# Holding back weight conversions and delaying squares in a seven-product feed-forward stage

## The chip, the cores and the metric

The kernel runs on 1 core of one Trainium2 chip. The metric is the device time of one execution in microseconds (us); the time of the kernel before is the median of three runs.

## The reference

Two groups of tokens (128 prompt tokens and 512 latent tokens, 640 in all, model width 1024) pass through two layers that share their weights:

```python
mod = silu(cond) @ w_ada + b_ada                  # shift, scale, gate for mixer and FFN
h = rmsnorm(x, g_pre_mix) * (1 + sc1) + sh1
z = h @ w_in                                      # all mixers' inputs and four branch gates
merged = sum(sigmoid(g[b]) * branch[b] for b in "ABCD")   # conv, pooling, short conv, attention
x = x + gt1 * rmsnorm(merged @ w_o, g_post_mix)
h = rmsnorm(x, g_pre_ffn) * (1 + sc2) + sh2
f = square(relu(h @ w_ff1)) @ w_ff2               # w_ff1 is 1024 x 4096
x = x + gt2 * rmsnorm(f, g_post_ffn)
```

All inputs are float32.

## The kernel before

**Precision by splitting.** Each float32 operand is held as a high part (a cast to the matmul type) and a low part (the rest), and each product is three matmuls: high x high, high x low, low x high (`mm3`, L247 to L256). For a weight, the high part `wh` is a ScalarE cast of the raw tile `wr` (L188) and the low part `wl` is a VectorE subtraction (L197). PE takes these two in that order: its first two matmuls of a block need `wh` alone, the third needs `wl`; where the weights are the moving operand (QKV and the `nat` products, L250 to L252) the second needs `wl`.

**Weight supply.** Weights come in units of 128x1024 through three raw buffers (`N_RAW`) and are converted into four sets of `wh` and `wl` (`N_SETS`). `w_pump` casts sets up to three ahead of the one in use (`SPLIT_AHEAD`) as far as sets are free, and notes each cast in the list `w_late`; `w_low` takes from that list and emits the low part and whatever follows from it. `w_pump` is called where a set is taken (`w_next`) and where one is given back (`w_done`). `w_low(1)` is called at the end of every `tick`, which also hands VectorE and ScalarE work of the side generators (convolution, attention, modulation) between PE's products. In `w_pump` a raw tile whose own or whose predecessor's low part is still in `w_late` first has that low part emitted, at once:

```python
while any(x[1] in (u, u - 1) for x in self.w_late):
    self.w_low(1)
```

The order of emission is the order on each engine; the queues are in order.

**Stages of a layer.** QKV blocks (two units each, three blocks); twelve *sections* (`section`, L1022: one unit, two halves of 24 matmuls of 320 columns each, and an evacuation after each half); the gate and branch products of four branches (`gp`, `bp`); `merged @ w_o` (`nat`); and the feed-forward in four quarters. A section is

```python
u, st = self.w_next()
for h in range(2):
    ps = self.mmps("sec")
    self.ws_half(ps, st, h, hi, lo)
    fn(h, slice(h * HALF, h * HALF + HALF), ps[:, :HALF])
    self.tick(1.76, KN['sec'])
self.w_done(u)
```

**The seven products.** The first quarter of the FFN is multiplied plainly. The other three (`ffn_pairs`, L1185; six calls in the program) form two 128-column blocks of w_ff1 for both token halves with seven products in place of eight, four such pairs per call. A pair takes four sets, here A to D: A serves products 1 and 2, B products 7 and 3, C (two halves, C1 and C2) products 5 and 6, D product 4. The sets C and D hold sums of weight blocks: two sums follow A's low part (L202, L203), one follows C1's (L205), one C2's (L208), and a set whose raw tile is such a sum can only be cast after it. After product 6 VectorE combines results in five operations (L1219 to L1223) into `U`; after product 4 one more finishes `R` (L1226). `square` is three ScalarE operations on 128x640 (Relu, Square, cast to `ghi`; L1195 to L1197), `low` a VectorE one (`glo`, L1202).

Of the kernel before, what the change touches and what calls it, by code (L numbers as in the profile page):

```python
# [24 lines left out]
SPLIT_AHEAD = 3  # L25
# [39 lines left out]
def r32(ap):  # L65
    return ap.bitcast(F32)
# [9 lines left out]
class Kernel:  # L76
# [95 lines left out]
    def w_pump(self, upto):  # L172
        nc = self.nc
        while self.w_split < len(self.parts) and self.parts[self.w_split][0] <= upto:
            i, c, u, rc, then = self.parts[self.w_split]
            if i not in self.w_set:
                if self.w_live >= N_SETS:
                    break
                self.w_set[i] = [self.wp.tile([128, 1024], F32R, tag=n, name=self.nm(n), bufs=N_SETS) for n in ("wh", "wl")]
                self.w_live += 1  # L180
            if u not in self.w_raw:
                self.w_low()
            while any(x[1] in (u, u - 1) for x in self.w_late):
                self.w_low(1)
            self.w_fetch(u)
            raw = self.w_raw[u][:, rc]
            hi, lo = [w[:, c] for w in self.w_set[i]]
            nc.scalar.copy(hi, raw)  # L188
            self.w_late.append((self.w_split, u, raw, hi, lo, then))
            self.w_split += 1  # L190
# [994 lines left out]
    def ffn_pairs(self, hi, lo, S, ghi, glo):  # L1185

        nc = self.nc
        v = nc.vector.tensor_tensor
        p, q = slice(0, HALF), slice(HALF, NTOK)
        acts = {1: [(hi[k][:, p], lo[k][:, p]) for k in range(4)], 2: [(hi[k][:, p], lo[k][:, p]) for k in range(4, 8)],  # L1190
                4: [(hi[k][:, q], lo[k][:, q]) for k in range(4, 8)], 3: S[4], 5: S[1], 6: S[2], 7: S[3]}
        late = []

        def square(j, x):
            nc.scalar.activation(x, x, AF.Relu)  # L1195
            nc.scalar.activation(x, x, AF.Square)
            nc.scalar.copy(ghi[j], x)  # L1197
            late.append((j, x))

        def low():  # L1200
            j, x = late.pop(0)
            v(glo[j], x, r32(ghi[j]), ALU.subtract)  # L1202

        for pr in range(4):
            U, R = self.T("u"), self.T("r")
            ps = {}
            for ns in ((1, 2), (7, 3), (5, 6), (4,)):
                u, st = self.w_next()
                for i, n in enumerate(ns):
                    w = ps[n] = (self.sdps if n in (7, 3, 5) else self.mmps)("ffp")[:, :HALF]  # L1210
                    for k in range(4):
                        c = slice(i * 512 + k * 128, i * 512 + k * 128 + 128)
                        self.mm3(w, st[0][:, c], st[1][:, c], *acts[n][k], k == 0, k == 3)
                    if n == 1:
                        nc.scalar.copy(U[:, p], w)
                    elif n == 2:
                        v(R[:, p], w, U[:, p], ALU.add)
                    elif n == 6:
                        v(U[:, p], w, U[:, p], ALU.add)  # L1219
                        v(R[:, q], ps[7], U[:, p], ALU.add)  # L1220
                        v(U[:, q], ps[5], R[:, q], ALU.subtract)
                        v(U[:, p], ps[5], U[:, p], ALU.subtract)
                        v(U[:, p], ps[3], U[:, p], ALU.add)  # L1223
                        square(2 * pr + 1, U)
                    elif n == 4:
                        v(R[:, q], w, R[:, q], ALU.add)  # L1226
                        square(2 * pr, R)
                    if late and n in (2, 3):
                        low()
                    self.credit = -1.0  # L1230
                    self.tick(0, 0)
                self.w_done(u)
        while late:
            low()
        self.credit = 0.0
# [287 lines left out]
```

## Time and profile before

| | before |
|---|---|
| median of 3 runs | 2097.64 us (2095.79 to 2099.55) |
| the profiled execution | 2097.92 us |
| its span, first to last instruction | 2096.2 us |
| PE busy | 2013.9 us (96%) |
| VectorE (DVE) busy | 1487.6 us (71%) |
| ScalarE (ACT) busy | 867.7 us (41%) |
| granted TensorE clock, mean | 0.988 |

The profile gives, for each engine, busy time and what it waited for. A matmul's duration overlaps with its successor's, so a gap in PE's work is read from the waits and the starts, and a stage's cost from the stretch between its first matmul and the first of the next stage.

### The profile page before, as it was taken

How to read it: one execution, taken by the hardware profiler on the slowest of the kernel's cores; microseconds unless marked ns; L12 is line 12 of the kernel's file. 1: busy time of each engine (PE TensorE's matmuls, PEld its weight loads, DVE VectorE, ACT ScalarE, POOL GpSimd, SP SyncE). 2: the span in 40 equal slices, each digit the busy share in tenths (PEclk: the TensorE clock that was granted, in tenths of full speed). 3: DMA queues.
4: the chain of work that ended last, by engine and by line, in shares of the span. 5: the costliest groups of instructions: out<-in, count | busy, mean ns of one | idle time of the engine just before them, and what ended most of it. 6: DMA issues, size and time to landing. Idle time of an engine off the chain costs nothing.

```text
span 2096.2 us, 30622 instructions
## 1 busy us (share of the span) xinstructions
PE 2013.9 (96%) x12080; PEld 1848.1 (88%) x12080; DVE 1487.6 (71%) x2597; ACT 867.7 (41%) x1618; POOL 293.9 (14%) x213
## 2 busy tenths in 40 slices
PE   7999999999999999999989999999999999999998
PEld 4999998899889888879789999989998888797886
DVE  4769876676678777677686798666875886646475
ACT  4543445442364351424354343545334543424251
POOL 1203001023131003040232050001221210100000
PEclk9999999999999999999999999999999999999999
DMA  7332121233433224242444222122334432313123
GB/s 301 120 101 80 61 76 46 91 116 122 151 131 116 86 95 143 73 128 90 152 138 134 63 73 75 60 88 71 121 121 161 141 103 69 121 51 101 41 88 124
DMA packets 77936, 221.40 MB, mean 106 GB/s; under 512 B 11224, under 2 KB 12248, under 8 KB 77792
## 3 DMA queue, kind: packets, MB, share of 16 engines
q1 hardware_dynamic: 48160, 164.00, 23.4%
q10 hardware_dynamic: 28096, 55.34, 8.2%
q8 instruction: 94, 1.54, 0.3%
q0 software_dynamic: 1536, 0.10, 0.3%
q14 instruction: 50, 0.41, 0.1%
HBM read 208.61 MB, written 10.80 MB: 105 GB/s over the span
## 4 chain that ended last, share of the span: by engine, by line
PE 65%; DVE 17%; ACT 9%; issue 4%; DMA 3%; POOL 2%; ACTq 0%; DVEq 0%; SPq 0%; POOLq 0%
PE nat L250 7%; PE nat L252 7%; PE nat L251 7%; PE gp L254 6%; PE gp L255 6%; PE gp L256 6%; DVE wl L197 5%; ACT wh L188 3%; PE sec L254 2%; PE sec L256 2%; PE sec L255 2%; PE bp L254 2%; PE bp L256 2%; PE bp L255 2%; DMA wa<-in_wada_dram 2%
## 5 line engine op out<-in xcount | busy, mean ns | idle before, releaser
L197 DVE TENSOR_TENSOR wl<-wr,wh 128x1024 fp32r<-128x1024 f32 (+1 forms) x336 | 392.0, 1172 | 251.6 <-ACT wh L188 249.7
L188 ACT CAST wh<-wr 128x1024 fp32r<-128x1024 f32 (+1 forms) x336 | 318.9, 958 | 371.9 <-PE nat L252 168.7
L254 PE MATMUL gp<-hhi,wh 128*128 128x320 f32 x1024 | 320.5, 313 | 0.0
L255 PE MATMUL gp<-hlo,wh 128*128 128x320 f32 x1024 | 317.8, 310 | 0.0
L256 PE MATMUL gp<-hhi,wl 128*128 128x320 f32 x1024 | 317.7, 310 | 0.0
L469 POOL PARTITION_ALL_REDUCE red<-acc x40 | 153.7, 3888 | 884.0 <-DVE acc L457 481.6
L250 PE MATMUL nat<-wh,ghi 128*128 128x512 f32 x640 | 254.1, 397 | 2.6 <-DVE r L1226 2.6
L251 PE MATMUL nat<-wl,ghi 128*128 128x512 f32 x640 | 253.5, 396 | 0.9 <-DVE wl L197 0.6
L252 PE MATMUL nat<-wh,glo 128*128 128x512 f32 x640 | 252.8, 395 | 0.0
L457 DVE SCALAR_TENSOR_TENSOR acc<-wa,silu_c,acc 128x512 f32<-128x512 f32 x280 | 195.4, 758 | 4.6 <-DMA wa<-in_wada_dram 4.5
L254 PEld LDWEIGHTS gp<-hhi,wh 128*128 128x128 f32 x1024 | 194.2, 190 | 1.2
L255 PEld LDWEIGHTS gp<-hlo,wh 128*128 128x128 f32 x1024 | 193.9, 189 | 1.2
L256 PEld LDWEIGHTS gp<-hhi,wl 128*128 128x128 f32 x1024 | 193.7, 189 | 0.0
L1118 ACT ACTIVATE sg<-gp 128x320 f32<-128x320 f32 x128 | 55.7, 436 | 283.6 <-PE gp L256 224.4
L250 PEld LDWEIGHTS nat<-wh,ghi 128*128 128x128 f32 x640 | 120.7, 189 | 32.9 <-DVE r L1226 5.2
L251 PEld LDWEIGHTS nat<-wl,ghi 128*128 128x128 f32 x640 | 120.6, 188 | 30.7 <-DVE wl L197 2.9
L252 PEld LDWEIGHTS nat<-wh,glo 128*128 128x128 f32 x640 | 120.6, 188 | 28.6
L863 DVE SCALAR_TENSOR_TENSOR cv<-val,wch,cv 128x113 f32<-128x113 f32 (+14 forms) x240 | 125.1, 588 | 0.1
L256 PE MATMUL ffp<-hhi,wl 128*128 128x320 f32 x384 | 120.2, 313 | 2.4 <-DVE wl L197 2.4
L254 PE MATMUL ffp<-hhi,wh 128*128 128x320 f32 x384 | 119.2, 311 | 1.4 <-ACT wh L188 1.4
L254 PE MATMUL sec<-hhi,wh 128*128 128x320 f32 x384 | 119.8, 312 | 0.0
L256 PE MATMUL sec<-hhi,wl 128*128 128x320 f32 x384 | 118.6, 309 | 0.0
(262 smaller groups left out, 4550.6 us busy)
## 6 DMA issues: line engine op xcount, KB each, us to landing
wr<-in_wu_dram SPq DMA_DIRECT2D x264, 512.0 KB, 3.7
wa<-in_wada_dram ACTq DMA_DIRECT2D x160, 256.0 KB, 3.1
wa<-in_wada_dram SPq DMA_DIRECT2D x16, 512.0 KB, 9.4
x<-x ACTq DMA_DIRECT2D x15, 512.0 KB, 3.3
x<-x SPq DMA_DIRECT2D x15, 512.0 KB, 4.9
x<-in_x_sample_dram SPq DMA_DIRECT2D x8, 512.0 KB, 6.3
gp<-in_g_post_dram ACTq DMA_DIRECT2D x16, 256.0 KB, 3.7
out_dram<-x SPq DMA_DIRECT2D x10, 256.0 KB, 2.0
```

Of the source, the lines that this page charges most:

```text
L188: nc.scalar.copy(hi, raw)
L197: v(lo, raw, r32(hi), ALU.subtract)
L250: mm(out, lhsT=xhi, rhs=whi, start=start, stop=False)
L251: mm(out, lhsT=xhi, rhs=wlo, start=False, stop=False)
L252: mm(out, lhsT=xlo, rhs=whi, start=False, stop=stop)
L254: mm(out, lhsT=whi, rhs=xhi, start=start, stop=False)
L255: mm(out, lhsT=whi, rhs=xlo, start=False, stop=False)
L256: mm(out, lhsT=wlo, rhs=xhi, start=False, stop=stop)
L457: nc.vector.scalar_tensor_tensor(acc[c], w[k], s, acc[c], ALU.mult, ALU.add)
L469: nc.gpsimd.partition_all_reduce(red[c], acc[c], 128, bass_isa.ReduceOp.add)
L863: nc.vector.scalar_tensor_tensor(y[:, lo:hi], u[:, lo + d:hi + d], w, y[:, lo:hi], ALU.mult, ALU.add)
L1118: nc.scalar.activation(sg[:, s], gp[:, :HALF], AF.Tanh, scale=0.5)
```

## The change

In `w_pump`, a set that is not yet due (`i >= self.w_at`, that is, not the one being taken) is no longer cast while the low part of its own or the preceding raw tile is still in `w_late`: the loop stops there until the next call. The due set is treated as before. In `ffn_pairs`, `w_pump` is called once more in front of each product; the squares of `U` and `R` go to a list `todo` and are emitted in front of products 4 and 2; and the low parts of `ghi` are emitted after products 1, 7 and 3 in place of 2 and 3.

```diff
@@ w_pump
         while self.w_split < len(self.parts) and self.parts[self.w_split][0] <= upto:
             i, c, u, rc, then = self.parts[self.w_split]
+            if i >= self.w_at and any(x[1] in (u, u - 1) for x in self.w_late):
+                break
             if i not in self.w_set:
                 if self.w_live >= N_SETS:
                     break
@@ ffn_pairs
-        late = []
+        late, todo = [], []
...
             for ns in ((1, 2), (7, 3), (5, 6), (4,)):
                 u, st = self.w_next()
                 for i, n in enumerate(ns):
+                    self.w_pump(self.w_at + SPLIT_AHEAD - 1)
+                    while todo and n in (4, 2):
+                        square(*todo.pop(0))
                     w = ps[n] = (self.sdps if n in (7, 3, 5) else self.mmps)("ffp")[:, :HALF]
...
                         v(U[:, p], ps[3], U[:, p], ALU.add)
-                        square(2 * pr + 1, U)
+                        todo.append((2 * pr + 1, U))
                     elif n == 4:
                         v(R[:, q], w, R[:, q], ALU.add)
-                        square(2 * pr, R)
-                    if late and n in (2, 3):
+                        todo.append((2 * pr, R))
+                    if late and n in (1, 7, 3):
                         low()
                     self.credit = -1.0
                     self.tick(0, 0)
                 self.w_done(u)
+        for x in todo:
+            square(*x)
         while late:
             low()
```

Two places show what moves. The first is ScalarE in a round of the seven-product stage, second pair of the first call. In the kernel before (`wh_7667` is the next pair's A, `wh_7702` its B, `wh_7740` its C1 and C2, `wh_7769` its D; `u` and `r` are U and R):

```order
L1215 COPY u_7632<-ffp_7637 128x320
L188 CAST wh_7667<-wr_7552 128x1024
L188 CAST wh_7702<-wr_7610 128x1024
L1195 ACTIVATE u_7632<-u_7632 128x640
L1196 ACTIVATE u_7632<-u_7632 128x640
L1197 CAST ghi_7486<-u_7632 128x640
L188 CAST wh_7740<-wr_7552 128x512 x2
L1195 ACTIVATE r_7633<-r_7633 128x640
L1196 ACTIVATE r_7633<-r_7633 128x640
L1197 CAST ghi_7485<-r_7633 128x640
L188 CAST wh_7769<-wr_7552 128x512
```

In the changed kernel ScalarE has, from the same copy on (`wh_7648` is this pair's own D, `wh_7669`, `wh_7704` and `wh_7739` the next pair's A, B and C):

```order
L1220 COPY u_7629<-ffp_7631 128x320
L190 CAST wh_7648<-wr_7294 128x512
L1197 ACTIVATE r_7500<-r_7500 128x640
L1198 ACTIVATE r_7500<-r_7500 128x640
L1199 CAST ghi_7483<-r_7500 128x640
L190 CAST wh_7669<-wr_7554 128x1024
L190 CAST wh_7704<-wr_7626 128x1024
L190 CAST wh_7739<-wr_7554 128x512
L1197 ACTIVATE u_7629<-u_7629 128x640
L1198 ACTIVATE u_7629<-u_7629 128x640
L1199 CAST ghi_7486<-u_7629 128x640
L190 CAST wh_7739<-wr_7554 128x512
```

The squares of `R` now belong to the pair before, D is cast in the pair that uses it, and C1 stands in front of the squares of `U`.

On VectorE the same round, from the last of the five combining operations to the first of the next pair, read before:

```order
L1223 TENSOR_TENSOR u_7632<-ffp_7688,u_7632 128x320
L197 TENSOR_TENSOR wl_7741<-wr_7552,wh_7740 128x512
L205 TENSOR_TENSOR wr_7552<-wr_7552,wr_7610 128x512
L1226 TENSOR_TENSOR r_7633<-ffp_7748,r_7633 128x320
L197 TENSOR_TENSOR wl_7741<-wr_7552,wh_7740 128x512
L208 TENSOR_TENSOR wr_7552<-wr_7552 128x512
L197 TENSOR_TENSOR wl_7770<-wr_7552,wh_7769 128x512
L1217 TENSOR_TENSOR r_7768<-ffp_7787,u_7767 128x320
```

and now:

```order
L1228 TENSOR_TENSOR u_7629<-ffp_7691,u_7629 128x320
L1231 TENSOR_TENSOR r_7630<-ffp_7745,r_7630 128x320
L199 TENSOR_TENSOR wl_7740<-wr_7554,wh_7739 128x512
L207 TENSOR_TENSOR wr_7554<-wr_7554,wr_7626 128x512
L1204 TENSOR_TENSOR glo_7494<-u_7629,ghi_7486 128x640
L199 TENSOR_TENSOR wl_7740<-wr_7554,wh_7739 128x512
L210 TENSOR_TENSOR wr_7554<-wr_7554 128x512
L1222 TENSOR_TENSOR r_7765<-ffp_7789,u_7764 128x320
```

`R` is finished ahead of C1's low part, the low part of `ghi` has moved up between C1 and C2, and D's low part is gone from here (it stands behind the last row).

The second place is in the mixer, which the diff does not name: the third and fourth section of layer 1. On ScalarE before (`sec_1272` is the second half of the third section, `sec_1305` and `sec_1358` the halves of the fourth, whose weights are `wh_971`; the cast `wh_1302` here is for `sec_1567`, three sections on):

```order
L1062 COPY val_1219<-sec_1272 128x320
L448 DMA wa_1300<-in_wada_dram 128x512
L188 CAST wh_1302<-wr_1009 128x1024
L448 DMA wa_1323<-in_wada_dram 128x512
L448 DMA wa_1332<-in_wada_dram 128x512
L1065 ACTIVATE sg_1220<-sec_1305 128x320
L448 DMA wa_1376<-in_wada_dram 128x512
L1065 ACTIVATE sg_1220<-sec_1358 128x320
```

and now (`sec_1256` is the second half of the third section, `sec_1298` and `sec_1343` the halves of the fourth):

```order
L1064 COPY val_1204<-sec_1256 128x320
L450 DMA wa_1284<-in_wada_dram 128x512
L450 DMA wa_1288<-in_wada_dram 128x512
L190 CAST wh_1292<-wr_960 128x1024
L450 DMA wa_1316<-in_wada_dram 128x512
L1067 ACTIVATE sg_1205<-sec_1298 128x320
L450 DMA wa_1339<-in_wada_dram 128x512
L450 DMA wa_1361<-in_wada_dram 128x512
L1067 ACTIVATE sg_1205<-sec_1343 128x320
L190 CAST wh_1379<-wr_1125 128x1024
```

PE at the border of these two sections before:

```order
L254 MATMUL sec_1272<-hhi_127,wh_963 128x320
L255 MATMUL sec_1272<-hlo_128,wh_963 128x320
L256 MATMUL sec_1272<-hhi_127,wl_964 128x320
L254 MATMUL sec_1305<-hhi_127,wh_971 128x320
L255 MATMUL sec_1305<-hlo_128,wh_971 128x320
L256 MATMUL sec_1305<-hhi_127,wl_972 128x320
```

and now:

```order
L256 MATMUL sec_1256<-hhi_127,wh_1201 128x320
L257 MATMUL sec_1256<-hlo_128,wh_1201 128x320
L258 MATMUL sec_1256<-hhi_127,wl_1202 128x320
L256 MATMUL sec_1298<-hhi_127,wh_1292 128x320
L257 MATMUL sec_1298<-hlo_128,wh_1292 128x320
L258 MATMUL sec_1298<-hhi_127,wl_1293 128x320
```

Before, `wh_971` had been cast ahead of the first section's first evacuation; now `wh_1292`, with which the fourth section begins, is cast behind the copy that reads the third section's last result.

## Rows read from the trace of the kernel before

**Rows 1.** The page: the span, and busy time of two engines.

```profile
span 2096.2 us, 30622 instructions
...
PE 2013.9 (96%) x12080; PEld 1848.1 (88%) x12080; DVE 1487.6 (71%) x2597; ACT 867.7 (41%) x1618; POOL 293.9 (14%) x213
```

**Rows 2.** Waits of PE: who waited for whom, us in total, times, longest us.

```profile
PE ffp L254 <- ACT wh L188: 19.5, 18, 1.7
...
PE qkv L251 <- DVE wl L197: 4.9, 4, 3.0
...
PE bp L254 <- DVE macc L1138: 2.2, 1, 2.2
...
PE ub L255 <- DVE plo L276: 2.1, 1, 2.1
```

**Rows 3.** Stretches: two seven-product calls and the sections of layer 1.

```profile
core 0: us, PE busy (x) PEld busy (x) DVE busy (x) ACT busy (x) POOL busy (x), PEclk, DMA share, GB/s
...
830.14:889.11 58.97, 54.92 (x339) 52.49 (x337) 42.01 (x65) 27.77 (x40) 0.00 (x0) 0.94 0.25 82
...
1747.31:1804.88 57.57, 52.78 (x339) 49.29 (x337) 37.08 (x57) 28.48 (x41) 0.00 (x0) 1.00 0.19 62
...
85.20:174.00 88.80, 88.80 (x625) 88.55 (x625) 66.15 (x162) 39.42 (x101) 3.53 (x10) 1.00 0.30 97
```

**Rows 4.** The chain through one round of the seven products: start, us, what.

```profile
1780.22 0.70 DVE wl L197
...
1781.68 0.62 ACT wh L188
...
1788.02 0.70 DVE wr L202
...
1789.51 1.07 ACT wh L188
...
1790.60 1.23 DVE wl L197
...
1793.71 0.50 DVE u L1223
...
1794.24 0.75 ACT u L1195
...
1795.78 0.73 ACT ghi L1197
...
1797.06 0.70 DVE wl L197
```

**Rows 5.** Groups of the same round: busy us, mean ns, idle before.

```profile
L1202 DVE TENSOR_TENSOR glo<-u,ghi 128x640 fp32r<-128x640 f32 x1 | 0.8, 818 | 0.0
```

**Rows 6.** Timeline at a section's half: start, us, engine, line, what.

```profile
105.15 0.31 PE L256 MATMUL sec<-hhi,wl 128*128 128x320 f32 x1
...
105.59 0.31 PE L256 MATMUL sec<-hhi,wl 128*128 128x320 f32 x1
...
105.99 0.43 ACT L1062 COPY val<-sec 128x320 f32<-128x320 f32 x1 [1.14 <-PE sec L256]
106.01 0.82 ACTq L448 DMA_DIRECT2D wa<-in_wada_dram  x2
```

**Rows 7.** Timeline at the start of the kernel, where a unit's weights come late.

```profile
37.84 0.38 PE L250 MATMUL qkv<-wh,hhi 128*128 128x256 f32 x1 [2.60 <-ACT wh L188]
...
39.10 0.39 PE L251 MATMUL qkv<-wl,hhi 128*128 128x256 f32 x1 [0.88 <-DVE wl L197]
```

**Rows 8.** Stretches right behind PE's gaps (columns as in rows 3).

```profile
39.70:43.10 3.40, 3.40 (x19) 3.40 (x18) 1.86 (x7) 3.40 (x12) 1.10 (x2) 0.50 0.77 249
196.70:200.10 3.40, 3.40 (x13) 3.40 (x14) 3.37 (x8) 0.33 (x2) 0.00 (x0) 0.50 0.38 124
1075.20:1078.60 3.40, 3.40 (x29) 3.40 (x30) 2.64 (x5) 1.32 (x3) 0.31 (x1) 1.00 0.70 189
1248.00:1251.40 3.40, 3.40 (x16) 3.36 (x15) 3.40 (x3) 0.31 (x1) 3.40 (x2) 0.50 0.18 43
```

## The prediction

> **What bounds the kernel now.** The page first: PE is busy for 96% of the span, VectorE for 71%, ScalarE for 41% [rows 1], so time can only be won where PE waits. PE's waits come next: the longest is in the seven products, 19.5 us for `wh` [rows 2]. Then the stretches: a seven-product call, from its first matmul to the first `nat` matmul that needs a low part, takes 57.57 us in layer 2 and up to 59 us in layer 1 [rows 3]. Three matmuls of 320 columns start within 0.44 us [rows 6], so a product of twelve takes 1.76 us and a call of 28 products 49.2 us: over 8 us of each of the six calls are waits. The chain through a round shows why: from one low part of C1 to the next, 1780.22 to 1797.06, it runs on VectorE and ScalarE alone, 16.84 us against 7 x 1.76 = 12.3 us of PE work per pair [rows 4]. In the sections it is the other way round: PE is busy without a gap at clock 1.00 while VectorE is at 66 of 88.8 us [rows 3]. Nothing can be won there, and every wait put in front of PE counts in full.
>
> **Part 1: the seven products.** The same operations run in another order, so only the loop changes. After the change it goes: cast D 0.62, squares of the former R 2.27 (from the start of the first to the cast behind the last, as those of U, 1794.24 to 1796.51), cast A 1.07, low A 1.23, two sums 1.40, cast B 1.07, low B 1.23, five combining operations 2.46 (0.49 each), squares of U 2.27, cast C2 0.62 with 0.2 more until the low part of `ghi` (0.82) lets VectorE go, low C2 0.70, sum 0.70 [rows 4, 5]. With a few hundredths for each hand-over that is 15.9 us a round, 0.9 us less than 16.84. It also starts more favourably: D's cast no longer waits for R's squares. In the first pair VectorE can combine only after six products (10.8 us); with the combining, squares of U, cast and low part of C2 and the sum, D of the second pair can be cast at about 17.6 us, that of the third at 33.5, of the fourth at 49.4. Three pairs then run without a wait (36.9 us); the fourth waits for A (low part at 38.7: 1.6 us), for 0.3 us at B, some 0.8 at C2 and D, and ends near 52.5. The first `nat` set is made 5.2 us after that D, at 54.7: this is where a call ends now, 2.9 us earlier than in layer 2, 4.3 us earlier than the two longer calls of layer 1. Six calls: 4 x 2.9 + 2 x 4.3 = 20 us. But each call keeps two waits of 1.6 to 2.2 us; gaps of that size before were followed by a slower clock in some calls (mean 0.94 against 1.00 in rows 3), so I take 5 us back: **-15 us**. Bounds -26 (six times 4.4) and 0.
>
> **Part 2: the sections, which the diff does not name.** The new test in `w_pump` holds for all units, and here it does harm. `w_done(i)` finds `w_late` empty, casts i+1 and must stop, since i+1's low part now pends; `w_next(i+1)` is called straight after it, stops at i+2 for the same reason, then emits i+1's low part; the ticks that follow find nothing to lower; and the next chance to cast is `w_done(i+1)`. Before, the pending low part was emitted and the cast went on, so that the sections ran on sets three units old. Once the reserve is used up, each unit is cast only after all of the previous one has been issued. Following `w_pump`, `w_next` and `w_done` through a layer, this holds from the sixth unit (second half of the third QKV block) over the twelve sections to the second gate product: 16 borders a layer. The order rows show one: `wh_1292` stands on ScalarE behind the copy of `sec_1256`.
>
> Price of a border: the copy starts 0.25 us after the next matmul could have (105.74, 105.99) and takes 0.43 [rows 6], the cast 1.07, the low part 1.23 [rows 4], hand-overs 0.1; PE has two matmuls (0.29) to do before it needs the low part: 2.75 us. The trace holds this chain once, at the start of the kernel: PE waits 2.60 us for the cast and 0.88 for the low part [rows 7], 3.48 us. Where the evacuation is VectorE's the cast needn't wait for it, which leaves 2.0 us. So 2.0 and 3.5 are the bounds, and I take 2.75. Work queued ahead of the low part adds to it where VectorE has more than 7 us to do in a section (key and value preparation, before the second section; the two short convolutions with the split of their results, before the first gate product) or ScalarE has softmax copies between evacuation and cast: by the counts in the order 1.8, 2.3, 1.7 and 0.7 us. DMA issues on ScalarE (0.82 us for two, [rows 6]) stand ahead of the cast at two borders: 1.6 us. QKV needs the unit only 1.4 us in, so that border costs 1.4; the last one 1.7, and 0.5 follows. Layer 1: 14 x 2.75 + 1.4 + 1.7 + 0.5 + 6.5 + 1.6 = 50 us; layer 2 has two more QKV borders, 53 us. At the second half of `merged @ w_o` the third set is now cast late: 0.8 us a layer. **+105 us**, bounds 75 and 135. VectorE and ScalarE lose nothing: their work is the same.
>
> **Part 3: the clock.** Of the four gaps of PE of 2 to 3.5 us that end at 39.1, 196.6, 1075.2 and 1246.5 us [rows 2, 7] three were followed by 3.4 us at a granted clock of 0.50, that is 1.2 GHz, and one ran on at 1.00 [rows 8]. 3.4 us at half speed cost 1.7. The 34 new gaps are of this size: three of four pay, 26 x 1.7 = 44, less 8 where VectorE's queue, not PE, sets the next border: **+36 us**, bounds 0 and 58.
>
> The Trainium skill has a rule that is sharper (TensorE: Matmul & The Clock Gate, HAM oscillation — how this bites in real kernels): in a kernel whose PE waited before every tile, the clock fell anew for each of them. By that rule all 34 borders pay, 58 us, and the sum is 2246; the trace agrees in three gaps of four and not in the one at 1075.
>
> **Sum.** The profiled execution took 2097.92 us, 0.3 over the median of three. 2097.9 - 15 + 105 + 36 = 2224 us.
>
> **The rivals.** (a) *The clock holds through the short gaps.* For it: the gap at 1075 [rows 8], and that each new gap is cut in two by a pair of matmuls. Against it: three of four. Then 2097.9 - 18 + 105 = 2185 us. (b) *Every border pays for the clock, and VectorE's queue adds more than counted*, since at 74% it has little room to recover: 2224 + 22 (58 less 36) + 12 for the queue = 2258 us. Its first half is the rule named in part 3. (c) *PE finds its weights ready at the borders*: ScalarE, 44% busy in the sections, would have to cast a unit before the former one ends. Place: each section's start; price: nothing, and the loop's gain is left, 2097.9 - 18 = 2080 us, faster. It decides below 15/34 = 0.45 us a border, less than the evacuating copy and its start alone (0.68). The order rows speak against it: the cast stands behind that copy. (d) *The loop does not get shorter*: freed sets, or raw tiles fetched later, hold the casts, and D's cast waits for PE in its own round. Then part 1 is nothing, 2239 us. Against it speaks that PE's waits in the round before are for the casts, none for a transfer [rows 2, 4].
>
> **How the numbers follow.** Forecast 0.53 (own range 2200 to 2250), (a) 0.20, (b) 0.15, (c) 0.05, (d) 0.07. The range from 2168 to 2275 takes in (a), (b), (d) and most of the bounds of part 2, and leaves out (c) and the tails, about 0.15. A measurement of this kernel can tell about 0.2%, 4 us, from no change: slower 0.94, same 0.01, faster 0.05.
>
> **What would show it.** Part 1 is right if the seven-product calls take 54 to 56 us, with the first wait of PE for `wh` near 37 us into a call instead of 33, and the round in the chain near 15.9 us. Part 2 is right if PE waits for `wh` and then `wl` at each start of a section (lines L256 and L258 of the changed kernel, some 24 times each for `sec`), and the sections of a layer take 125 to 145 us in place of 89. Part 3 is right if the granted clock in that stretch falls to about 0.89 and the rest keeps its level; at 1.00 it is (a), at 0.85 or below (b). It is wrong altogether if PE is still busy without a gap in the sections.

## The result and the profile after

The changed kernel takes 2210.59 us in the median (2207.96 to 2214.13, 4 runs) where the kernel before takes 2098.6 (2095.79 to 2100.71, 4 runs): ratio 1.0536, 95% interval 1.0516 to 1.0556, slower. The forecast was 2224, the range 2168 to 2275. The profiled execution took 2214.13 us.

The page of the changed kernel, which answers to [rows 1]: the span, and busy time.

```profile
span 2212.2 us, 30598 instructions
...
PE 2044.8 (92%) x12080; PEld 1868.0 (84%) x12080; DVE 1496.7 (68%) x2597; ACT 867.4 (39%) x1618; POOL 279.7 (13%) x213
```

PE's idle time is the span less its busy time: 82.3 us before, 167.4 now. And 30.9 us more are "busy" although the matmuls are the same. That agrees with the granted clock, which within the span is 0.50 for 49.4 us before and for 112.0 us now: half of the difference is 31.3 us. VectorE is busy 9.1 us longer, ScalarE as long as before.

Waits of PE in the changed kernel, which answer to [rows 2] (who waited for whom: us in total, times, longest):

```profile
PE sec L256 <- ACT wh L190: 39.3, 20, 4.4
PE sec L258 <- DVE wl L199: 26.5, 24, 3.6
PE gp L258 <- DVE wl L199: 14.9, 8, 4.2
PE bp L258 <- DVE wl L199: 10.6, 2, 5.4
...
PE ffp L258 <- DVE wl L199: 7.2, 14, 0.7
...
PE ffp L256 <- ACT wh L190: 2.3, 6, 0.7
```

The 19.5 us for `wh` that headed the list before are down to 2.3. In their place stand the sections (`sec`), which did not wait at all, the first gate products (`gp`) and the first branch products (`bp`).

Stretches, as [rows 3] has them: two seven-product calls up to the first `nat` matmul that needs a low part, then the sections of layer 1 and of layer 2, from the first matmul to the end of the last; and two stretches behind borders in the sections (the number behind POOL's is the granted clock).

```profile
896.57:952.28 55.71, 52.00 (x339) 49.37 (x337) 43.29 (x67) 28.47 (x42) 0.00 (x0) 1.00 0.26 81
1875.40:1929.71 54.31, 51.42 (x339) 49.33 (x337) 40.55 (x60) 29.05 (x42) 3.76 (x2) 1.00 0.21 68
88.66:228.21 139.55, 107.70 (x647) 101.65 (x648) 72.53 (x169) 37.63 (x100) 3.61 (x10) 0.91 0.20 66
1186.83:1327.38 140.55, 108.82 (x647) 102.69 (x648) 74.86 (x173) 37.48 (x100) 3.61 (x10) 0.90 0.19 61
141.00:144.40 3.40, 3.40 (x15) 3.40 (x15) 1.97 (x7) 0.00 (x0) 0.00 (x0) 0.50 0.36 141
117.40:120.80 3.40, 2.70 (x22) 2.45 (x21) 1.49 (x2) 0.39 (x1) 0.00 (x0) 1.00 0.44 136
```

The calls are 3 us shorter than in [rows 3], at clock 1.00. The sections take some 140 us in each layer; in the kernel before, from the same first to the same last matmul, they took 92.65 and 92.23. About 32 us of each 140 are idle, and PE is 15 to 17 us longer busy.

One border of two sections, from the timeline of the changed kernel (start, us, engine, line, what; the idle time ahead in brackets):

```profile
148.30 0.31 PE L258 MATMUL sec<-hhi,wl 128*128 128x320 f32 x1
148.65 0.43 ACT L1077 COPY sb<-sec 128x320 f32<-128x320 f32 x1 [1.26 <-PE sec L258]
148.97 1.05 ACT L190 CAST wh<-wr 128x1024 fp32r<-128x1024 f32 x1
150.05 1.23 DVE L199 TENSOR_TENSOR wl<-wr,wh 128x1024 fp32r<-128x1024 f32 x1 [2.45 <-ACT wh L190]
150.07 0.41 PE L256 MATMUL sec<-hhi,wh 128*128 128x320 f32 x1 [1.46 <-ACT wh L190]
...
151.33 0.63 PE L258 MATMUL sec<-hhi,wl 128*128 128x320 f32 x1 [0.70 <-DVE wl L199]
```

This is an ordinary border in six lines. ScalarE takes the evacuating copy, and only behind it the cast of the weights with which PE should go on; then VectorE's low part. Measured from start to start, against a matmul every 0.146 us, PE loses 1.62 and 0.86 us here, 2.49 us before rounding; the idle times in brackets, 1.46 and 0.70, are shorter because a matmul's duration overlaps with the next one's.

The round of the seven products, from one low part of A (128x1024) to the next one in the call at 1875:

```profile
1896.96 1.23 DVE L199 TENSOR_TENSOR wl<-wr,wh 128x1024 fp32r<-128x1024 f32 x1
...
1912.70 1.22 DVE L199 TENSOR_TENSOR wl<-wr,wh 128x1024 fp32r<-128x1024 f32 x1
```

15.74 us a round in place of the 16.84 of [rows 4].

### The profile page after: what moved, and what is told of

It is laid out like the page before. It is cut to its first block, busy times and chain, and to the rows that moved or that the text cites. A ratio compares the mean times of both kernels' runs of the same rounds, so it can differ in the third digit from the quotient of the medians.

```text
span 2212.2 us, 30598 instructions
## 1 busy us (share of the span) xinstructions
PE 2044.8 (92%) x12080; PEld 1868.0 (84%) x12080; DVE 1496.7 (68%) x2597; ACT 867.4 (39%) x1618; POOL 279.7 (13%) x213
## 5 line engine op out<-in xcount | busy, mean ns | idle before, releaser
L471 POOL PARTITION_ALL_REDUCE red<-acc x40 | 141.6, 3585 | 798.1 <-DVE acc L459 546.0
L459 DVE SCALAR_TENSOR_TENSOR acc<-wa,silu_c,acc 128x512 f32<-128x512 f32 x280 | 196.8, 761 | 10.5 <-DMA wa<-in_wada_dram 10.5
L256 PE MATMUL sec<-hhi,wh 128*128 128x320 f32 x384 | 130.2, 339 | 39.3 <-ACT wh L190 39.3
L258 PE MATMUL sec<-hhi,wl 128*128 128x320 f32 x384 | 129.6, 338 | 26.5 <-DVE wl L199 26.5
L257 PE MATMUL sec<-hlo,wh 128*128 128x320 f32 x384 | 126.1, 328 | 0.0
```

What stands on the lines that cost most here:

```text
L256: mm(out, lhsT=whi, rhs=xhi, start=start, stop=False)
L257: mm(out, lhsT=whi, rhs=xlo, start=False, stop=False)
L258: mm(out, lhsT=wlo, rhs=xhi, start=False, stop=stop)
L459: nc.vector.scalar_tensor_tensor(acc[c], w[k], s, acc[c], ALU.mult, ALU.add)
L471: nc.gpsimd.partition_all_reduce(red[c], acc[c], 128, bass_isa.ReduceOp.add)
```

## The experiments

Ratios are to the kernel before on the same chip, with 95% intervals. Line numbers move by a few with each edit.

**1. The test, in the pairs alone.** The new test holds only while the seven products are being issued.

```
-            if i >= self.w_at and any(x[1] in (u, u - 1) for x in self.w_late):
+            if self.hold and i >= self.w_at and any(x[1] in (u, u - 1) for x in self.w_late):
...
+        self.hold = True
         for pr in range(4):
...
+        self.hold = False
         for x in todo:
```

> The changed kernel, with its new test in the weight pump active only inside the seven-product function; everywhere else the pump works as before the change. Theory (the loss comes from the test in the sections, the gain from the seven products): the sections of layer 1 take about 89 us again at a granted clock of 1.00, the six seven-product calls stay at 52.4 to 54.5 us from first to last matmul, and the time is 2098.6 less about 21 to 26: 2073 to 2078 us. Rival (the later squares and casts hurt in other places too, or the shorter calls owe something to the late weights around them): the sections recover but the calls do not stay short, 2090 to 2105 us.

Measured: 2070.55 us, ratio 0.9884 (0.9862 to 0.9907); the range was reckoned from 2098.6 us, and on this chip the kernel before takes 2093.68. The sections of layer 1 and a call of layer 2:

```profile
85.88:178.50 92.62, 92.62 (x652) 92.39 (x651) 70.06 (x167) 39.83 (x103) 3.70 (x10) 1.00 0.29 94
1732.66:1786.93 54.27, 51.47 (x338) 49.36 (x337) 38.06 (x58) 28.53 (x41) 0.00 (x0) 1.00 0.21 68
```

PE is busy without a gap through the sections again, and the calls stay short: the loss is the test outside the pairs. (The sections take 92.6 us as before the change; the 89 us that I expected come from a stretch that ends short of their last matmul.) The page of this kernel sets the two costs apart:

```profile
span 2069.4 us, 30617 instructions
...
PE 2001.4 (97%) x12080; PEld 1839.8 (89%) x12080; DVE 1490.8 (72%) x2597; ACT 867.1 (42%) x1618; POOL 290.6 (14%) x213
```

68.0 us idle. The changed kernel has 167.4 - 68.0 = 99.4 us more of it, and 2044.8 - 2001.4 = 43.4 us more of busy PE.

**2. The test alone**, added to the kernel before.

```
             i, c, u, rc, then = self.parts[self.w_split]
+            if i >= self.w_at and any(x[1] in (u, u - 1) for x in self.w_late):
+                break
```

> The kernel before with nothing added but the test in the weight pump, active everywhere; the squares and the pumps in the seven products stay as they were. Theory (the test alone starves the sections and gives nothing in the seven products): all of the loss without the gain, sections as in the changed kernel (PE waits of about 1.6 us for wh and 0.9 us for wl at each border), calls no shorter than the 57 us of before, 2225 to 2245 us. Rival (the test itself shortens the seven-product calls, the squares and pumps only help): calls of 53 to 55 us and about the time of the changed kernel, 2205 to 2215 us.

Measured: 2232.56 us, ratio 1.0662 (1.0642 to 1.0682). PE's waits:

```profile
PE sec L256 <- ACT wh L190: 39.4, 20, 4.5
PE sec L258 <- DVE wl L199: 26.6, 24, 3.6
PE ffp L256 <- ACT wh L190: 20.1, 22, 1.7
```

All of the loss, and in the seven products nothing: PE waits there for `wh` as it did before (20.1 us against 19.5), and the six calls, up to the first `nat` low part, sum to 348.1 us as against 348.3.

**3. Without the test.** The changed kernel with the two lines of the test taken out.

> The changed kernel without the test in the pump: only the later squares and the pump in front of each product are left. Theory (the gain in the calls is the new order of squares and casts, for which the test is not needed): sections at 89 us, calls at 52.4 to 54.5 us, 2073 to 2080 us. Rival (without the test a cast waits for a low part that is put in front of it on VectorE at once, so the sums come earlier and the gain is lost): calls at 56 to 58 us, 2095 to 2100 us.

Measured: 2065.69 us, ratio 0.9865 (0.9846 to 0.9884), a little better than expected. Call and sections:

```profile
1731.18:1784.99 53.81, 51.13 (x339) 49.39 (x337) 38.08 (x58) 28.22 (x41) 0.00 (x0) 1.00 0.21 69
85.89:178.50 92.61, 92.61 (x651) 92.36 (x650) 70.02 (x167) 39.81 (x103) 3.71 (x10) 1.00 0.29 94
```

The gain needs no test; the calls are even 0.5 us shorter than with it. Nor does it need the pump in front of each product: without the test, that call finds nothing to do, because `w_next` has just pumped to the same limit and no set comes free before `w_done` (this is read from the code; no run takes that line out alone). What is left of the change is the later squares, with the place of their low parts. Beside the kernels of experiment 6 it was timed once more:

> The changed kernel without the test once more, beside the two halves and the next kernel: both squares later, calls of 51.8 us in layer 2, ratio to before 0.985 to 0.989.

Measured: 2067.63 us, ratio 0.9855 (0.9842 to 0.9867). This version beats both kernels.

**4. The test everywhere, and a pump more.** One call at the end of `tick`, behind the low part that it puts out:

```
         self.w_low(1)
+        self.w_pump(self.w_at + SPLIT_AHEAD - 1)
```

> The changed kernel with its test kept for all units, and one call more: the weight pump is also tried at the end of every tick, right after the tick has put out one pending low part. Theory (the test does harm only because no later call finds the pending list empty in time, so that the look-ahead runs down to zero): with a cast possible after every tick the sections find their weights ready, no wait for wh at section borders, 89 to 95 us from the first section to the first gate product at clock 1.00, calls of 52 to 54.5 us, and the time of the kernel with the test in the pairs alone, 2065 to 2080 us. Rival (holding a cast back behind its predecessor's low part is itself too late in the sections, whoever calls the pump): waits for wh or wl stay, above 2130 us.

Measured: 2079.27 us (2076.47 to 2086.54), ratio 0.9926 (0.9908 to 0.9944). Sections of layer 1:

```profile
85.61:177.07 91.46, 91.46 (x646) 91.30 (x645) 69.09 (x167) 39.10 (x102) 3.73 (x10) 1.00 0.32 100
```

The test still holds for every unit here, and the sections lose nothing. So it isn't the holding back that costs; it is that nothing pumps between the moment the pending low part is put out and the end of the unit. The 0.4% to the kernel of experiment 1 lie outside the sections and calls. In the profiled execution, the slowest of six, PE waits 5.7 us for `xn` at the start of layer 2, where experiment 1 has 2.1 in two waits (this wait is taken up under the next heading); what else makes them up was not followed.

**5. The clock: work in place of the gaps.** First ten matmuls in front of each section unit, that need no new weights:

```
                 ps = self.mmps("sec")
+                for _ in range(10 if h == 0 else 0):
+                    nc.tensor.matmul(ps[:, :HALF], lhsT=self.identr, rhs=hi[0][:, :HALF], start=True, stop=True)
```

> The changed kernel with ten more matmuls of 128x320 in front of each of the 24 section units, into the bank that the section overwrites afterwards; they need no new weights and take 10 x 0.146 = 1.46 us, a little less than the 1.6 us for which PE waits there, so they replace idle time by work. Theory (short gaps are followed by a lower clock, which costs time on top of the wait): the 78 us at a granted clock of 0.5 in the two stretches of sections and first gate products shrink to less than 40, and the kernel is faster by 10 to 25 us although PE has 240 matmuls more, 2185 to 2200 us. Rival (the low clock there falls on time that PE would wait anyway): no change, 2208 to 2213 us. Second rival (the clock falls because of the waits for wl, which stay): low time as before and up to 8 us slower where the extra matmuls run at half speed.

Measured: 2207.72 us, ratio 1.0546 (1.0523 to 1.0569), no different from the changed kernel's 1.0536 on another chip, though the mean granted clock of the profiled execution, the fastest of four, is 0.982 for 0.975. So it was run again beside the changed kernel, together with one in which the gap for `wl` is filled too, by five matmuls whose zero weight adds nothing (`fill` is 10 and 5 in a section's first half, 8 and 5 at the first two gate units):

```
             if k == 0 and fill[1]:
                 mm(out[:, :HALF], lhsT=st[0][:, c], rhs=hi[k][:, s], start=True, stop=False)
                 mm(out[:, :HALF], lhsT=st[0][:, c], rhs=lo[k][:, s], start=False, stop=False)
+                for _ in range(fill[1]):
+                    mm(out[0:32, :HALF], lhsT=self.zeror, rhs=hi[k][:, s], start=False, stop=False)
                 mm(out[:, :HALF], lhsT=st[1][:, c], rhs=hi[k][:, s], start=False, stop=False)
```

> The changed kernel as it is, once more, on the same chip as the next three, so that they can be compared with it directly: 1.053 to 1.055 of the time before by every theory, some 70 us at a granted clock of 0.5 in the two stretches from the first section to the third gate product.

> The kernel with ten matmuls in front of each section unit again, now beside the changed kernel. In its first profile the low clock in the sections fell from 72 to 41 us and the span was 11 us shorter, but its median was no better than the changed kernel's on another chip. Theory (the low clock after gaps costs time of its own): 8 to 14 us below the changed kernel. Rival (it falls on time that PE would wait for the next weights anyway): within 4 us of it.

> As the kernel before, and in addition five matmuls with a zero weight of 32 columns (128x320, 0.146 us each, they add nothing) between the wait for wh and that for wl, and the same 8 and 5 at the first two gate units: nearly all the idle time of the short borders is now work, 412 matmuls more. Theory (the clock's share of the loss is about 31 us of half-speed work in the whole kernel, nearly all of it here): below 20 us at a granted clock of 0.5 in the sections, and 20 to 28 us below the changed kernel, 2180 to 2190. Rival (the borders are bound by the chain copy, cast, low part, whatever PE's clock): low time gone, time within 5 us of the changed kernel.

Measured on one chip: changed kernel 2210.71 us, ratio 1.0545 (1.0531 to 1.0558); borders filled 2209.15, 1.0541 (1.0527 to 1.0554); both waits filled 2204.08, 1.0513 (1.0499 to 1.0527). The last is faster by 6.6 us than the changed kernel, though it has 412 matmuls more; the one with borders filled can't be told from it. Both expected gains were too large. The sections of both layers, the changed kernel's first, then with both waits filled:

```profile
88.02:225.77 137.75, 105.88 (x647) 99.86 (x648) 72.54 (x169) 37.62 (x100) 3.61 (x10) 0.93 0.21 66
1184.24:1324.93 140.69, 108.84 (x647) 102.72 (x648) 74.85 (x173) 37.48 (x100) 3.61 (x10) 0.90 0.20 61
```

```profile
87.12:224.24 137.12, 127.91 (x829) 119.75 (x828) 72.58 (x169) 39.03 (x102) 3.61 (x10) 0.96 0.21 67
1177.44:1315.08 137.64, 128.88 (x829) 121.13 (x828) 74.89 (x173) 38.87 (x102) 3.86 (x10) 0.95 0.19 63
```

24 x 15 added matmuls of 0.146 us are 52.6 us; without them PE is busy for 256.8 - 52.6 = 204.2 us, against 214.7. So a higher clock gives 10.5 us back, as work at half speed would. But idle time fell by only 45.7 us (63.7 to 18.0) for the 52.6: at four borders PE did not wait for `wh` in the first place, and there the filling itself is a delay of 4 x 1.46 us. What remains at 0.50 lies behind the waits that the filling doesn't cover, 1.9 to 5.4 us long. The two stretches of sections are 3.7 us shorter in all, 9.5 us without that delay. The 6.6 us of the medians can't be put down to the clock as a whole: of the 8.4 us between the two profiled executions 3.4 stand at the start of layer 2, where PE waits 5.1 us for `xn` in the one and 1.7 in the other, in code that the edit doesn't touch.

**6. Which squares.** The kernel without the test and without the pump that has nothing to do there, with only U's squares later (`todo.append` for U, `square` at once for R), and with only R's.

> The kernel before, without the test; of the squares in the seven products only those of U come one product later (behind the casts of C1 and C2), those of R stay in front of the cast of D. Theory (the gain is that C1's and C2's casts no longer stand behind the 2.27 us of squares of U, which are on the chain of the round): most of the gain of the kernel without the test, calls of 52 to 54 us, ratio to before 0.987 to 0.990. Rival (the squares of R in front of D's cast close the round): calls at 55.5 to 57 us, 0.995 to 1.000.

> The other half: only the squares of R come later (into the next pair, behind its first product), so that D's cast goes ahead of them; those of U stay in front of the casts of C1 and C2. Theory (U's squares are on the chain, R's beside it): little, calls of 55.5 to 57 us, ratio 0.995 to 1.000. Rival (R's squares close the round): 52 to 54 us, 0.987 to 0.990. If both halves come out near the middle, the two are needed together.

Measured: U's later 2076.35 us, ratio 0.9900 (0.9887 to 0.9913); R's later 2111.87 us, ratio 1.0066 (1.0054 to 1.0079). Low parts of A, one pair after the other, with U's later:

```profile
1755.67 1.22 DVE L197 TENSOR_TENSOR wl<-wr,wh 128x1024 fp32r<-128x1024 f32 x1
...
1771.71 1.22 DVE L197 TENSOR_TENSOR wl<-wr,wh 128x1024 fp32r<-128x1024 f32 x1
```

and with R's later, with the squares of U ahead of C's cast between:

```profile
1777.20 1.23 DVE L197 TENSOR_TENSOR wl<-wr,wh 128x1024 fp32r<-128x1024 f32 x1
...
1784.67 0.74 ACT L1195 ACTIVATE u<-u 128x640 f32<-128x640 f32 x1 [3.67 <-DVE u L1225]
...
1786.21 0.72 ACT L1197 CAST ghi<-u 128x640 fp32r<-128x640 f32 x1
1786.84 0.61 ACT L188 CAST wh<-wr 128x512 fp32r<-128x512 f32 x1
1787.48 0.69 DVE L197 TENSOR_TENSOR wl<-wr,wh 128x512 fp32r<-128x512 f32 x1 [2.85 <-ACT wh L188]
...
1795.19 1.23 DVE L197 TENSOR_TENSOR wl<-wr,wh 128x1024 fp32r<-128x1024 f32 x1
```

Rounds of 16.04 and 17.99 us, against 16.84 before and 15.59 with both. U's squares are on the chain: the cast of C stands behind them, and VectorE waits 2.85 us for it. Moved alone, R's squares go from a place where they are hidden to one in front of A's cast: both squares are then on the chain. Only after U's are gone does moving R's help, by another 0.45 us a round. For U the time came as expected, though not the calls (54.6 to 57.4 us from first to last matmul for 52 to 54); for R the theory and the rival both had the wrong sign.

**7. VectorE relieved.** The low parts of the squares of three pairs on GpSimd:

```
-            v(glo[j], x, r32(ghi[j]), ALU.subtract)
+            (v if j > 5 else nc.gpsimd.tensor_tensor)(glo[j], x, r32(ghi[j]), ALU.subtract)
```

> As the kernel before, with one thing more: the low parts of the squares (glo, 0.82 us each on VectorE) of the first three pairs of a call are made on GpSimd, those of the last pair stay on VectorE. Theory (VectorE, with about 12.3 us of work in a round that takes 15 to 16, is what the loop runs on): 1.6 us a round less on VectorE, the fourth pair waits less, calls of 50 to 51 us, 6 to 10 us less than the kernel without the test. Rival (GpSimd slows VectorE down while both work, or ScalarE's casts close the round): calls at 51.5 to 52.5 us and the same time.

Measured: 2077.93 us, ratio 0.9909 (0.9896 to 0.9922): 10 us slower than without it, calls of 53.6 to 55.0 us from first to last matmul, longer than theory and rival had them; the low parts of A come every 16.10 us (1757.17, 1773.27) in place of 15.59. The trace shows why under the last heading.

## Why the prediction came out right, step by step

In the profiled executions the sum can be set against the forecast part by part, with the kernel of experiment 1 as the step between: spans 2096.2, 2069.4, 2212.2. One wait has to be set apart first. At the start of layer 2 PE waits for the normalised input `xn`, and behind that stands a VectorE operation that waits for the transfer of the modulation values (`mc`). In the kernel before, in experiment 1 and in the changed kernel PE waits there for (us in total, times, longest):

```profile
PE hT L553 <- ACT xn L537: 5.6, 1, 5.6
```

```profile
PE hT L556 <- ACT xn L540: 2.1, 2, 1.5
```

```profile
PE hT L555 <- ACT xn L539: 5.2, 1, 5.2
```

The kernel of experiment 3 has 3.1 us in one of its two profiles and 1.6 in the other, so this wait isn't the same in every execution of a kernel; what makes it long or short was not followed. It puts 3.5 us (5.6 less 2.1) into part 1 below and 3.1 us into part 2 that belong to neither mechanism.

**Part 1, forecast -15, measured -26.8** (-23.1 in the medians of experiment 1). The mechanism was right and its sizes too: a round of 15.74 us for 15.9, the first wait for `wh` 37.3 us into a call of layer 2 (up to 39.5 in layer 1) for "near 37", the end of a call at 54.3 to 56.5 for 54 to 56. The six calls sum to 329.5 us instead of 348.3, 18.8 less (328.4 in experiment 1, 19.9 less), where I had 20 before the clock. The step that failed is the 5 us that I took back for the clock: the waits that are left, 0.25 and 0.70 us here where I had 1.6 to 2.2, are followed by no slow stretch, and the granted clock is 1.00 in all six calls.

```profile
1912.72 0.41 PE L256 MATMUL ffp<-hhi,wh 128*128 128x320 f32 x1 [0.25 <-ACT wh L190]
...
1913.98 0.41 PE L258 MATMUL ffp<-hhi,wl 128*128 128x320 f32 x1 [0.70 <-DVE wl L199]
```

Rather than fall, the clock rose: in the kernel before, four of the six calls hold 20.5 us at 0.50 between them, in the changed kernel none does. What that is worth is not shown. In the kernel before, the call at 716 holds 3.41 us of it and takes 57.57 us, no more than the calls at 1747 and 1861, which hold none. Of the 26.8 us, 19.9 are the calls and 3.5 the wait at the start of layer 2; the kernel before also has 6.83 us at 0.50 there and experiment 1 none, which may be most of the 3.4 that are left. The step where I let D's cast ahead of R's squares count as a gain of its own was wrong too: experiment 6 shows that alone it loses.

**Part 2, forecast +105, measured +99.4 of idle time** (+96.3 in experiment 2 against before: 178.6 less 82.3; 3.1 of the 99.4 are the wait at the start of layer 2). PE waits for `wl` at all 24 starts of a section and for `wh` at 20. An ordinary border costs 2.49 us for the 2.75 of the forecast. The waits of layer 1 between 88 and 265 us sum to 50.6 us for 50, which is partly luck: the first gate and branch products were dearer than I had them. At the worst, four convolution steps stand ahead of the low part, 5.23 us from 243.18 on:

```profile
248.34 1.21 DVE L199 TENSOR_TENSOR wl<-wr,wh 128x1024 fp32r<-128x1024 f32 x1
...
249.60 0.63 PE L258 MATMUL bp<-zh,wl 128*128 128x320 f32 x1 [5.27 <-DVE wl L199]
```

A wait of 4.2 us that I did not foresee stands at 572 us, in the last gate products of layer 1, where VectorE has products for the modulation (2.74 us) and a sum (2.25 us) ahead of a low part.

**Part 3, forecast +36, measured +43.4** of busy PE (+36.9 in experiment 2). The clock of the sections is 0.91 and 0.90 for the 0.89 forecast. "Three of four gaps pay" was a poor description all the same. In the changed kernel's trace the twelve waits for weights with 3.1 us and more of idle time were all followed, or overlapped, by a stretch at 0.50, some of them by 6.8 us of it; of the eighteen shorter borders of sections, 1.4 to 2.8 us of idle time, six were (the rows at 141 and 117 us above show one of each). By the rule of the Trainium skill that I had named (TensorE: Matmul & The Clock Gate, HAM oscillation — how this bites in real kernels) each wait of a repeated pattern pays; its example has waits of some 3 to 5 us. The trace agrees for the long waits and not for two thirds of the short ones. That the low clock is a cost of its own is shown by experiment 5, for the part that could be filled: 10.5 us of PE's busy time. That the other 33 us are of the same kind is worked out, not shown: the clock is 0.50 for 112.0 us within the span of the changed kernel and for 31.0 in experiment 1, and half of the difference is 40.5 of the 43.4 us.

The sum: -26.8 + 99.4 + 43.4 = 116.0 for the 126 forecast (112 in the medians). That it comes within 10 us is in part luck: the parts are off by -11.8, -5.6 and +7.4, and the last takes back part of the other two. In rivals (a) and (c) the loop's gain stands as 18 us without a working; by part 1 it is 20, which changes nothing that was decided. Rival (c), the only one on the fast side, fell with the border above: the cast does stand behind the evacuating copy. Rival (d) fell with the calls, (a) with the clock; of (b) the queue of VectorE came true in a few places, the clock at six of eighteen short borders.

What the forecast did not see is how the change hangs together. The text of the diff reads as if the test made room for the later squares. Experiments 2 and 3 show that the test gives nothing in the calls, and with it gone the added pumps have nothing to do: the gain, 1.3 to 1.5%, is that of the later squares with their low parts, and the loss, 6.6%, that of the test alone; 138.9 - 28.0 = 110.9 us in the medians, nearly the 112 of the change.

## What to carry to other kernels

A guard in a shared helper that stops work "until the pending piece is out" takes away look-ahead wherever no later call retries in time; before adding one, follow the helper's callers through the stages that the change isn't about, and limit the guard or add the retry. On a loop over two engines' queues, find which long operation stands between a result and the next cast, and move that one first: moved alone, the other one may go from a hidden place onto the chain. And a bundle of edits is worth taking apart even when its sum is understood: here one of its parts held all of the gain.

## What the runs showed of the hardware

GpSimd's work slowed VectorE's. In experiment 7, with one low part of a square on GpSimd beside one low part of weights on VectorE, twice in a round:

```profile
1769.35 1.58 POOL L1202 TENSOR_TENSOR glo<-u,ghi 128x640 fp32r<-128x640 f32 x1 [11.51 <-ACT ghi L1197]
1769.83 1.65 DVE L197 TENSOR_TENSOR wl<-wr,wh 128x512 fp32r<-128x512 f32 x1 [1.27 <-ACT wh L188]
...
1772.37 1.56 POOL L1202 TENSOR_TENSOR glo<-r,ghi 128x640 fp32r<-128x640 f32 x1 [1.44 <-ACT ghi L1197]
1773.27 1.74 DVE L197 TENSOR_TENSOR wl<-wr,wh 128x1024 fp32r<-128x1024 f32 x1 [1.40 <-ACT wh L188]
```

The same operations take 0.69 and 1.23 us where GpSimd rests. Here they end 0.55 and 1.08 us after GpSimd's do, 0.14 and 0.15 us less than their undisturbed times, as if all but a short beginning came only then; so it is in all 36 such pairs of the trace. VectorE loses 0.96 + 0.51 us a round and was relieved of 1.65: almost nothing is won, and what is lost lies on the chain. The whole kernel's VectorE time is 1489.6 us with, and 1489.0 without the relief. The Trainium skill has this rule (SBUF — State Buffer, Who interferes with whom): a VectorE instruction with two SBUF inputs contends with a GpSimd instruction that reads SBUF, the ports that they share are an exclusive lock, and the order of issue decides which of the two blocks. The 36 pairs agree with it: VectorE's operation came second each time.

The other is how little an idle gap of PE tells of the clock: gaps of 2.49 us, cut in two by a pair of matmuls, were followed by a granted clock of 0.50, that is 1.2 GHz, behind some borders and by 1.00 behind others, with the same work on PE before and after. The twelve longer waits of the changed kernel were all followed or overlapped by 0.50, but length alone doesn't settle it. In the two profiles of experiment 3's kernel, on two chips, the first QKV block of layer 2 waits equally long for its low part, and the clock behind the wait is 1.00 in the first and 0.50 in the second (in experiment 1, after 3.21 us, 1.00):

```profile
1059.28 0.38 PE L251 MATMUL qkv<-wl,hhi 128*128 128x256 f32 x1 [3.21 <-DVE wl L197]
1060.00:1064.00 4.00, 4.00 (x37) 4.00 (x36) 3.25 (x8) 2.60 (x4) 0.55 (x1) 1.00 0.79 239
```

```profile
1058.29 0.58 PE L251 MATMUL qkv<-wl,hhi 128*128 128x256 f32 x1 [3.22 <-DVE wl L197]
1060.00:1064.00 4.00, 4.00 (x21) 4.00 (x20) 3.25 (x8) 2.68 (x5) 0.55 (x1) 0.50 0.67 225
```
